# Where the stationary operands begin: 76 bytes instead of 88 or 0 into their buffers

## The chip, the cores and the metric

The kernel runs on one core of a Trainium2 chip. The metric is the time of one execution on the device in microseconds; the median of three runs is given, and beside it the profile of one execution of its own.

## The reference

One layer of a decoder trunk, x of 256 positions by 1024 features, all in float32. `proj = x @ w_in` is ten matrices of 1024 x 1024 side by side: `a_x, a_gate, s_u, s_v, q, k, v, g_a, g_s, g_m`.

- Branch A: a causal convolution of width 4 over a_x, then two gates r and i from eight 128 x 128 blocks each, `sigmoid(x @ w_r + b_r)` and the same with w_i, a linear recurrence over the positions, and a product with `gelu(a_gate)`.
- Branch B: `gelu(s_u)` times a causal 128 x 128 mixing over positions of the layer-normed `gelu(s_v)`.
- Branch C: with 256 positions and blocks of 256 this is plain causal attention with 8 heads of 128.

`merged = sigmoid(g_a) y_a + sigmoid(g_s) y_s + sigmoid(g_m) y_m`, then `x = LN(alpha x + merged @ w_out)`, then `x = LN(alpha x + ffn(x))`, where ffn has an up projection to 2 x 3072 features (gate and up), a convolution of width 3 on the gate half, gelu, product, and a down projection.

## The kernel before, in words

All large products are made in three passes of a faster float format: each operand is split into a high part `hi` (a cast on ScalarE, L70) and a low part `lo` (the difference, on VectorE, L71), and TensorE adds `hi*hi + hi*lo + lo*hi` (`passes`, L125). Weights come in chunks of 1 MB (128 partitions by 2048 numbers). A chunk is loaded into two `raw` buffers by `load` (L86, DMA queue of SyncE) and split by `prep` (L101) into one `hi` and one `lo` buffer; there are four of each, and chunks are loaded and split up to three chunks ahead of the step that uses them (`LOOK`).

TensorE's work is a list of steps in an order written out by hand (L917 on), and TensorE runs them in that order; ScalarE, VectorE and GpSimd have a planner's order, except around the first layer norm and at the end. A step is the matmuls (`pe`) and what follows them on other engines (`post`). There are these kinds:

- Feature-major steps (`fm_pe`, L219): a_x, s_u, a_gate, g_m, q, k, g_a, g_s, and the up projections of the feed-forward part. A chunk of weights is the stationary operand, 128 columns at a time, and the activations are the moving operand, 256 columns. One step is 48 matmuls at L229 (two output halves, three passes, eight blocks of k). There are 32 of them in the input projection, with x's parts `xh, xl` moving, and 22 in the feed-forward part with `x1Th, x1Tl` moving.
- Wide steps (s_v, v, w_out, down): the weights are moving, 512 columns, and the activations stationary.
- The r/i steps (`ri_step`, L410): six matmuls each, eight steps in four pairs, between the four g_m steps. Stationary are the blocks of `rg_hi, rg_lo`, moving the convolved a_x.
- Attention: scores, transposes, and `pv_step` (L562), where the halves of V, `avh, avl`, are stationary for six of ten matmuls.
- The first two gate chunks (`first_gates`, L774), where the shifted chunks are moving; constant `TM`.

Where a chunk's weights begin in its buffer is set per chunk: `shifted(i, by)` (L236) notes a number of bytes and `prep` cuts the 2048 numbers out of a buffer that is `PAD` numbers longer. Input's feature-major chunks have `FM_IN`, 88 bytes, the feed-forward's `FM_UP`, 76 bytes, all others 0. Larger activations, rg and V stand in ten slots of 8192 bytes per partition with the tag U, made by the helper `U` (L66); they begin at byte 0 of their slot. All buffers begin at multiples of 128 bytes or, for the smallest, of 32.

Of the kernel before, what the change touches and what calls it, by code (L numbers as in the profile page):

```python
# [1 line left out]

# [5 lines left out]
F32 = mybir.dt.float32  # L8
F32R = mybir.dt.float32r
# [7 lines left out]
P = 128  # L17
D = 1024
S = 256
KT = D // P  # L20
# [23 lines left out]

FM_IN, FM_UP, TM = 88, 76, 76
PAD = 256


@with_exitstack
def trunk_kernel(ctx: ExitStack, tc, xT, x, w_in, wrg, wsT, w_out, w_up, w_down, rows, packed, out):
# [7 lines left out]
    up = ctx.enter_context(tc.tile_pool(name="up", bufs=10))  # L60
# [2 lines left out]
    psa = ctx.enter_context(tc.tile_pool(name="psa", bufs=4, space=bass.MemoryType.PSUM))  # L63
    psb = ctx.enter_context(tc.tile_pool(name="psb", bufs=4, space=bass.MemoryType.PSUM))

    def U(name, shape=(P, KT, S), dt=F32):  # L66
        return up.tile(list(shape), dt, name=name, tag="U")

    def split(src, hi, lo, sub=nc.vector):
        nc.scalar.copy(hi, src)  # L70
        sub.tensor_sub(lo, src, hi.bitcast(F32))  # L71
# [14 lines left out]
    def load(i):  # L86

        parts = loaded[i] = []
        if i == 0:
            loaded["x"] = U("xraw")  # L90
        raw = [raws.tile([P, 1024], F32, name=f"raw{i}{h}", tag="raw") for h in range(2)]
        w = 512 if i < 4 else 1024
        for at in range(0, 2048, w):
            k = 2 * i + at // 1024 if i < 4 and at % 1024 == 0 else None
            if k is not None:
                nc.sync.dma_start(loaded["x"][:, k, :], xT[:, k, :])
            r = raw[at // 1024][:, at % 1024 : at % 1024 + w]
            nc.sync.dma_start(r, chunks[i][:, at : at + w])
            parts.append((r, slice(at, at + w), k))

    def prep(i):  # L101
        at = shift_of.get(i, 0) // 4
        hi = his.tile([P, 2048 + PAD], F32R, name=f"hi{i}", tag="hi")[:, at : at + 2048]
        lo = los.tile([P, 2048 + PAD], F32R, name=f"lo{i}", tag="lo")[:, at : at + 2048]
        ready[i] = (hi, lo)
# [172 lines left out]


    va = U("va", (P, 2, D))  # L280
    vst = small.tile([P, 2, 2, 6], F32, name="vst", tag="vst", bufs=1)
    psv = {}

    def sv_post():
        gb = U("gb", (P, 2, D))
        load_row(gb[:, 0, :], 0)
        load_row(gb[:, 1, :], 1)
        for tok in range(2):
            for h in range(2):
                nc.scalar.activation(va[:, tok, HALVES[h]], psv[tok, h], AF.Gelu_apprx_tanh)  # L290
                nc.vector.bn_stats(vst[:, tok, h, :], va[:, tok, HALVES[h]])
        for tok in range(2):
            mv, rs = aggregate(vst[:, tok], f"sv{tok}")
            normalise(va[:, tok, :], va[:, tok, :], mv, rs, gb[:, 0, :], gb[:, 1, :])
# [18 lines left out]
    rg = {}  # L313

    def load_rg():
        hi = U("rg_hi", (P, 2, KT, P), F32R)
        lo = U("rg_lo", (P, 2, KT, P), F32R)
        for m in range(2):
            raw = raws.tile([P, KT, P], F32, name=f"rg_raw{m}", tag="raw")
            nc.sync.dma_start(raw.rearrange("p g j -> p (g j)"), wrg[:, m * D : (m + 1) * D])  # L320
            split(raw, hi[:, m], lo[:, m])
        rg["h"], rg["l"] = hi, lo
# [142 lines left out]
    av = {}  # L465
# [1 line left out]
    pv = {}  # L467

    def v_post():
        av["h"] = U("avh", (P, 2, D), F32R)  # L470
        av["l"] = U("avl", (P, 2, D), F32R)
        av["r"] = U("avr", (P, D))
        for tok in range(2):
            for h, s in enumerate(HALVES):
                split(pv[tok, h], av["h"][:, tok, s], av["l"][:, tok, s])
                if tok == 1:
                    nc.scalar.copy(av["r"][:, s], pv[tok, h])

    def v_step(c):
        wide_step(V_, c, "p_v", pv, v_post)  # L480
# [439 lines left out]
    ax_step(0)  # L920
    ax_step(1)
    post_only(load_rg)
    ax_step(2)
    ax_step(3)
# [168 lines left out]
```

## Time and profile before

| | us |
|---|---|
| median of 3 runs | 480.73 |
| lowest, highest | 479.95, 480.8 |
| profiled execution | 479.52 |
| its span, first to last instruction | 477.6 |

The granted clock is 0.995 of the full one over the span. By the page, TensorE is busy for 98% of the span, VectorE for 70%, ScalarE for 57%. The feature-major line L229 and the row line L635 hold most of TensorE's time. In the timeline of an engine, a row is a run of equal instructions that follow one another: its start, the time from the first's start to the last's end, and how many. The rows of two runs overlap, since matmuls are pipelined; so the distance between two starts is the measure of how fast TensorE gets on, not the busy time.

### The profile page before, as it was taken

How to read it: one execution, taken by the hardware profiler on the slowest of the kernel's cores; microseconds unless marked ns; L12 is line 12 of the kernel's file. 1: busy time of each engine (PE TensorE's matmuls, PEld its weight loads, DVE VectorE, ACT ScalarE, POOL GpSimd, SP SyncE). 2: the span in 40 equal slices, each digit the busy share in tenths (PEclk: the TensorE clock that was granted, in tenths of full speed). 3: DMA queues.
4: the chain of work that ended last, by engine and by line, in shares of the span. 5: the costliest groups of instructions: out<-in, count | busy, mean ns of one | idle time of the engine just before them, and what ended most of it. 6: DMA issues, size and time to landing. Idle time of an engine off the chain costs nothing.

```text
span 477.6 us, 8706 instructions
## 1 busy us (share of the span) xinstructions
PE 467.3 (98%) x3536; PEld 443.6 (93%) x3536; DVE 336.3 (70%) x519; ACT 271.5 (57%) x400; POOL 21.8 (5%) x24
## 2 busy tenths in 40 slices
PE   8999999999999999999999999999999999999993
PEld 6899999999889999999998899999999999999983
DVE  4799989464389868676685988765666556666635
ACT  5665775576795577577451478545544454444431
POOL 1002000000000000000000800000000000000003
PEclk9999999999999999999999999999999999999998
DMA  7996868574522875765452449766556566555002
GB/s 243 355 349 247 276 209 271 182 242 150 175 82 102 251 267 184 241 245 168 141 178 90 152 139 324 276 216 202 189 178 204 196 181 212 182 185 185 26 0 88
DMA packets 27959, 92.91 MB, mean 195 GB/s; under 512 B 3216, under 2 KB 4624, under 8 KB 27920
## 3 DMA queue, kind: packets, MB, share of 16 engines
q1 hardware_dynamic: 27920, 92.37, 58.3%
q8 instruction: 27, 0.44, 0.4%
q14 instruction: 12, 0.10, 0.1%
HBM read 91.31 MB, written 1.05 MB: 193 GB/s over the span
## 4 chain that ended last, share of the span: by engine, by line
issue 46%; PE 46%; DVE 3%; ACT 1%; DMA 1%; POOL 1%; SPq 0%; ACTq 0%; DVEq 0%; POOLq 0%
PE p_u L229 14%; PE p_d L635 13%; PE p_g L229 11%; PE p_sv L265 4%; PE p_tg L247 2%; PE p_ax L229 1%; DMA raw<-in_w_in 1%; PE p_dq L635 1%; ACT hi L70 1%; DVE lo L71 0%; DVE va L206 0%; DVE st_m L193 0%; POOL rs_sv L201 0%; DVE x1Tl L71 0%; POOL rs_m L201 0%
## 5 line engine op out<-in xcount | busy, mean ns | idle before, releaser
L71 DVE TENSOR_TENSOR lo<-raw,hi 128x1024 fp32r<-128x1024 f32 (+1 forms) x165 | 191.3, 1183 | 71.4 <-ACT hi L70 70.7
L70 ACT CAST hi<-raw 128x1024 fp32r<-128x1024 f32 (+1 forms) x167 | 162.9, 1008 | 100.9 <-PE p_g L229 26.3
L635 PE MATMUL p_d<-hi,act 128*128 128x512 f32 x180 | 55.6, 390 | 0.0
L635 PEld LDWEIGHTS p_d<-hi,act 128*128 128x128 f32 x180 | 33.0, 188 | 6.3
L635 PE MATMUL p_d<-lo,act 128*128 128x512 f32 x90 | 35.0, 389 | 0.0
L329 DVE SCALAR_TENSOR_TENSOR cv<-p_g,par,cv 128x255 f32<-128x255 f32 (+1 forms) x48 | 23.1, 480 | 7.1 <-ACT cv L327 6.3
L229 PE MATMUL p_u<-x1Th,hi 128*128 128x256 f32 x192 | 26.0, 278 | 0.0
L229 PE MATMUL p_u<-x1Th,lo 128*128 128x256 f32 x192 | 25.7, 276 | 0.0
L229 PE MATMUL p_u<-x1Tl,hi 128*128 128x256 f32 x192 | 25.7, 276 | 0.0
L229 PEld LDWEIGHTS p_u<-x1Th,hi 128*128 128x128 f32 x192 | 24.5, 188 | 0.8
L327 ACT ACTIVATE cv<-p_g,par 128x256 f32<-128x256 f32 x24 | 13.5, 562 | 19.9 <-DVE cv L329 19.8
L229 PEld LDWEIGHTS p_u<-x1Th,lo 128*128 128x128 f32 x192 | 23.6, 188 | 0.0
L229 PEld LDWEIGHTS p_u<-x1Tl,hi 128*128 128x128 f32 x192 | 23.5, 188 | 0.0
L767 DVE TENSOR_TENSOR cv<-cv,p_u 128x512 f32<-128x512 f32 x12 | 8.2, 687 | 19.2 <-PE p_u L229 19.2
L229 PE MATMUL p_g<-x1Th,lo 128*128 128x256 f32 x160 | 21.4, 276 | 0.0
L229 PE MATMUL p_g<-x1Th,hi 128*128 128x256 f32 x160 | 21.4, 276 | 0.0
L229 PE MATMUL p_g<-x1Tl,hi 128*128 128x256 f32 x160 | 21.4, 276 | 0.0
L635 PEld LDWEIGHTS p_d<-lo,act 128*128 128x128 f32 x90 | 16.9, 188 | 3.6
L229 PEld LDWEIGHTS p_g<-x1Th,lo 128*128 128x128 f32 x160 | 19.6, 188 | 0.0
L229 PEld LDWEIGHTS p_g<-x1Th,hi 128*128 128x128 f32 x160 | 19.6, 188 | 0.0
L229 PEld LDWEIGHTS p_g<-x1Tl,hi 128*128 128x128 f32 x160 | 19.6, 188 | 0.0
L751 ACT ACTIVATE cv<-cv 128x512 f32<-128x512 f32 x12 | 7.6, 632 | 11.3 <-DVE cv L329 11.3
(242 smaller groups left out, 934.8 us busy)
## 6 DMA issues: line engine op xcount, KB each, us to landing
raw<-in_w_in SPq DMA_DIRECT2D x72, 512.0 KB, 5.3
raw<-in_w_up SPq DMA_DIRECT2D x48, 512.0 KB, 4.6
raw<-in_w_down SPq DMA_DIRECT2D x24, 512.0 KB, 4.9
raw<-in_w_in SPq DMA_DIRECT2D x16, 256.0 KB, 5.2
raw<-in_w_out SPq DMA_DIRECT2D x8, 512.0 KB, 3.9
xraw<-in_xT SPq DMA_DIRECT2D x8, 128.0 KB, 4.7
gb<-in_rows SPq DMA_DIRECT2D x2, 512.0 KB, 6.6
rg_raw<-in_wrg SPq DMA_DIRECT2D x2, 512.0 KB, 6.9
```

The costliest lines, as they stand in the source:

```text
L70: nc.scalar.copy(hi, src)
L71: sub.tensor_sub(lo, src, hi.bitcast(F32))
L229: nc.tensor.matmul(dst[:, j, :], w[:, k, j * P : (j + 1) * P], a[:, k, :], start=(n == 0), stop=(n == 3 * KT - 1))
L247: nc.tensor.matmul(dst, a[:, k, tok * P : (tok + 1) * P], w[:, k, :], start=(m == 0 and k == 0), stop=(m == 2 and k == KT - 1))
L265: nc.tensor.matmul(tiles[tok, h], a[:, 2 * c + k, tok * P : (tok + 1) * P], w[:, k, HALVES[h]], start=(c == 0 and k == 0 and m == 0), stop ...
L327: nc.scalar.activation(dst, src, AF.Identity, bias=pcol(bname, f), scale=w(taps - 1))
L329: nc.vector.scalar_tensor_tensor(dst[:, d:], src[:, : S - d], w(taps - 1 - d), dst[:, d:], op0=ALU.mult, op1=ALU.add)
L635: nc.tensor.matmul(dst, a[:, k0 + k, tok * P : (tok + 1) * P], w[:, k, s], start=(start and n == 0), stop=(stop and n == 6 * len(parts) - 1))
L751: nc.scalar.activation(t, t, AF.Gelu_apprx_tanh)
L767: nc.vector.tensor_mul(t, t, pf["u", c])
```

## The change

`FM_IN` becomes 76. A new constant `STAT`, 76, is the byte at which rg's and V's high and low parts begin in their slots; for that `U` takes a number of bytes, makes each slot 2048 + 32 numbers long, cuts the wanted numbers out and gives them their shape. `PAD` goes from 256 to 128 numbers. All buffers behind the first pair of weight buffers come to stand elsewhere, the slots of U 8320 bytes apart in place of 8192.

```diff
-FM_IN, FM_UP, TM = 88, 76, 76
-PAD = 256
+FM_IN, FM_UP, TM = 76, 76, 76
+
+STAT = 76
+PAD = 128
...
-    def U(name, shape=(P, KT, S), dt=F32):
-        return up.tile(list(shape), dt, name=name, tag="U")
+    def U(name, shape=(P, KT, S), dt=F32, by=0):
+
+        t = up.tile([P, 2048 + 32], dt, name=name, tag="U")[:, by // 4 : by // 4 + math.prod(shape[1:])]
+        axes = "abcd"[: len(shape) - 1]
+        return t.rearrange(f"p ({' '.join(axes)}) -> p {' '.join(axes)}", **dict(zip(axes, shape[1:])))
...
-        hi = U("rg_hi", (P, 2, KT, P), F32R)
-        lo = U("rg_lo", (P, 2, KT, P), F32R)
+        hi = U("rg_hi", (P, 2, KT, P), F32R, STAT)
+        lo = U("rg_lo", (P, 2, KT, P), F32R, STAT)
...
-        av["h"] = U("avh", (P, 2, D), F32R)
-        av["l"] = U("avl", (P, 2, D), F32R)
+        av["h"] = U("avh", (P, 2, D), F32R, STAT)
+        av["l"] = U("avl", (P, 2, D), F32R, STAT)
```

## Rows read from the trace of the kernel before

**Rows 1.** The page, parts 1 and 2: busy time of engines, granted clock by slice.
```profile
PE 467.3 (98%) x3536; PEld 443.6 (93%) x3536; DVE 336.3 (70%) x519; ACT 271.5 (57%) x400; POOL 21.8 (5%) x24
...
PEclk9999999999999999999999999999999999999998
```

**Rows 2.** TensorE's waits: for whom, us in total, times, longest.
```profile
PE p_x1t L675 <- DVE x L725: 0.7, 1, 0.7
PE p_su L229 <- DVE xc L329: 0.3, 1, 0.3
```

**Rows 3.** TensorE's timeline (start, us, line, matmuls), fast steps: second a_x, first g_m.
```profile
33.41 1.07 PE L229 MATMUL p_ax<-xh,hi 128*128 128x256 f32 x8
...
38.85 1.07 PE L229 MATMUL p_ax<-xh,hi 128*128 128x256 f32 x8
...
97.83 1.07 PE L229 MATMUL p_gm<-xh,hi 128*128 128x256 f32 x8
...
103.28 0.28 PE L416 MATMUL p_ri<-xch,rg_hi 128*128 128x256 f32 x1
```

**Rows 4.** The same timeline, second u step and its successor.
```profile
55.65 1.20 PE L229 MATMUL p_su<-xh,hi 128*128 128x256 f32 x8 [0.32 <-DVE xc L329]
...
61.48 1.06 PE L377 MATMUL p_mix<-ws_raw,va 128*128 128x128 f32 x8
```

**Rows 5.** The same timeline: second g_m step, from behind one r/i pair to the next.
```profile
104.71 1.10 PE L229 MATMUL p_gm<-xh,hi 128*128 128x256 f32 x8
...
110.31 0.28 PE L416 MATMUL p_ri<-xch,rg_hi 128*128 128x256 f32 x1
```

**Rows 6.** The same timeline: first a_gate step, first g_s step, each with its successor.
```profile
75.02 1.19 PE L229 MATMUL p_ag<-xh,hi 128*128 128x256 f32 x8
...
80.58 1.05 PE L377 MATMUL p_mix<-ws_raw,va 128*128 128x128 f32 x8
...
224.12 1.18 PE L229 MATMUL p_gs<-xh,hi 128*128 128x256 f32 x8
...
229.80 0.40 PE L569 MATMUL p_o<-pT,avh 128*128 128x256 f32 x2
```

**Rows 7.** Stretches: us, TensorE busy (matmuls), granted clock, DMA share, GB/s.
```profile
33.41:38.84 5.43, 5.43 (x50) 1.00 1.02 404
104.71:110.30 5.59, 5.59 (x50) 1.00 0.67 215
```

**Rows 8.** TensorE's timeline, feed-forward: u steps behind transposes and behind a down step.
```profile
283.64 1.19 PE L229 MATMUL p_u<-x1Th,hi 128*128 128x256 f32 x8
...
289.21 0.60 PE L809 MATMUL p_g<-ident,tg 128*128 128x128 f32 x4
...
306.03 1.08 PE L229 MATMUL p_u<-x1Th,hi 128*128 128x256 f32 x8
...
311.48 1.07 PE L229 MATMUL p_g<-x1Th,hi 128*128 128x256 f32 x8
```

**Rows 9.** Timelines of ScalarE, then TensorE, around the start of V's projection.
```profile
123.66 2.00 ACT L70 CAST hi<-raw 128x1024 fp32r<-128x1024 f32 x2 [3.09 <-PE p_gm L229]
...
127.12 0.49 ACT L424 ACTIVATE i<-p_ri,par 128x256 f32<-128x256 f32 x1
...
126.76 0.62 PE L265 MATMUL p_v<-lo,xh 128*128 128x512 f32 x2
127.22 0.94 PE L265 MATMUL p_v<-hi,xh 128*128 128x512 f32 x2
```

**Rows 10.** TensorE's timeline, one step of probabilities times V and its successor.
```profile
194.56 0.40 PE L569 MATMUL p_o<-pT,avh 128*128 128x256 f32 x2
...
195.73 0.39 PE L512 MATMUL p_s<-kf,qf 128*128 128x128 f32 x2
```

**Rows 11.** VectorE's groups by line, 82 to 103 us, then 300 to 440 us.
```profile
L71 DVE TENSOR_TENSOR lo<-raw,hi 128x1024 fp32r<-128x1024 f32 x8 | 9.5, 1221 | 2.7 <-ACT hi L70 2.7
...
L71 DVE TENSOR_TENSOR lo<-raw,hi 128x1024 fp32r<-128x1024 f32 x53 | 63.2, 1221 | 30.7 <-ACT hi L70 30.6
```

More of the change, by code (lines that the diff above doesn't have):

```diff
@@ L1 @@
+import math
 from contextlib import ExitStack
```

## The prediction

> **What bounds the kernel now.** I read part 1 and part 2 of the page first: TensorE is busy for 98% of the span and its clock is at the upper level (2.4 GHz) in every slice but the last [rows 1]. The waits of TensorE came next: the longest inside the input projection is 0.3 us, for the convolution on VectorE in front of the second u step, and the one for the second layer norm's rows in front of the transposes 0.7 us [rows 2]. So nearly all the time is the spacing of matmuls, and the question is whether that spacing is the same wherever the same instruction runs. For this I took TensorE's timeline and divided the distance between the starts of two steps by the matmuls between them. One feature-major step is 48 matmuls of 256 columns, with the weights stationary and the activations moving.
>
> The second a_x step takes 38.85 - 33.41 = 5.44 us, the first g_m step 103.28 - 97.83 = 5.45 us: 113.3 ns a matmul [rows 3]. The second u step, with the same 48 instructions and the same 88 bytes, takes 61.48 - 55.65 = 5.83 us, 121.5 ns a matmul with a long first distance of some 0.2 us in it and 120 ns without [rows 4]. The three later g_m steps take 110.31 - 104.71 = 5.60 us (the first of three equal ones), 116.7 ns a matmul, and the r/i steps around them, whose weights begin at byte 0 of their slots, take (104.71 - 103.28) / 12 = 119 ns [rows 5]. The first g_s step takes 229.80 - 224.12 = 5.68 us where the first a_gate step, which also follows 128-column matmuls, takes 80.58 - 75.02 = 5.56 us [rows 6]. So there are three spacings, 113, 117 and 120 ns, and once a step has a slow one it keeps it. It isn't the clock, which is granted in full in both, nor the DMA: the fast step ran beside 404 GB/s, a slow one beside 215 GB/s [rows 7].
>
> The feed-forward steps have their weights 76 bytes in. The first u step there, entered after transposes as the first g_s step is, begins with a block that is 0.12 us longer and then settles: 289.21 - 283.64 = 5.57 us; after a down step it is 311.48 - 306.03 = 5.45 us [rows 8]. I found no step with 76 bytes stationary that stays slow, among 22 of them; with 88 bytes five of 32 do (the second u, three g_m, one g_s), and with 0 bytes every r/i step.
>
> **The change part by part.** It adds no instruction and no transfer. It moves three things: the start of 32 weight chunks from byte 88 to 76, the start of the r/i weights and of V's two halves from byte 0 to 76, and, through the smaller pad and the larger slots, the base of all buffers behind the first pair. The bases stay multiples of 128 bytes.
>
> *The second u step.* Its entry is dear anyway (the wait, then a long first distance), so I don't take 5.44 but the 5.56 us of the first a_gate step: 5.83 - 5.56 = 0.27 us. Ends: 0 if it stays at 120 ns, 0.39 at the full 5.44.
>
> *The g_m steps.* Three times 5.60 - 5.44 = 0.48 us. They follow the r/i steps and seem to inherit their slowness. Ends: 0 and 0.48; I take 0.48, since both the matmuls before them and they themselves move to the offset of [rows 8].
>
> *The r/i steps.* 48 matmuls from about 119.7 to 113.3 ns: 0.30 us. Ends: 0 and 0.30. Of this the last pair is not kept. After it the V projection waits for a PSUM bank that ScalarE frees: two casts from 123.66 on (released by TensorE's last reading of the weights two thirds through the last g_m step), then a sigmoid and four more at 0.36 us. TensorE's first block after that is 0.94 us in place of 0.62 [rows 9]. ScalarE's chain doesn't shorten, so TensorE only comes some 0.1 us earlier to the same wait: minus 0.10.
>
> *The first g_s step.* 5.68 - 5.56 = 0.12 us. Ends 0 and 0.12.
>
> *Probabilities times V.* A step is ten matmuls in 195.73 - 194.56 = 1.17 us [rows 10]; six have V's halves stationary, of which two or three come before the 128-column pair that breaks the rhythm. Four steps with two matmuls at 6.7 ns less give 0.05 us. Ends: 0 and 24 x 6.7 ns = 0.16 us.
>
> *Writing at another offset.* VectorE's subtraction into a weight buffer takes 1221 ns at 88 bytes and 1221 ns in the feed-forward part, where 76 and 0 bytes alternate [rows 11]; I cost the writes at nothing, and what hides them anyway is that TensorE never waits for a weight buffer there. If VectorE were late, the second u step's wait of 0.3 us would grow first.
>
> Two statements of the Trainium skill speak against this. "TensorE: Matmul & The Clock Gate", section "Step-by-step: what each phase is for", says that TensorE reads moving and stationary operands through two independent ports, so that loading the next weights takes nothing from the running matmul; by that the bytes could not matter and the sum would be 0. The trace disagrees so far as the same instruction has three spacings, 113, 117 and 120 ns [rows 3 to 6]. "SBUF — State Buffer", section "Specifications (TRN2)", says that memory is read in lines of 16 bytes and that every crossing costs; 76 isn't a multiple of 16, so that by it the r/i weights and V would read one line more and lose, and the sum would be at most 0.87 us without these two. Here too the trace disagrees: the weights at byte 0 have the longest spacing, 119 ns [rows 5].
>
> **Sum:** 0.27 + 0.48 + 0.30 - 0.10 + 0.12 + 0.05 = 1.12 us. TensorE is what ends last before and after, so the saving reaches the end of the span, and the layer norms, which hang on TensorE's last matmul before them, move along. The profiled execution has a span of 477.6 and took 479.52 us, 1.2 us under the median of 480.73; the saving is taken off the median: 479.6 us.
>
> **The rivals.** *Entry decides, not the bytes.* With 88 bytes eight steps entered after 128-column matmuls settle, the first a_gate step [rows 6] being one of them, so the slow ones may be accidents of the phase at which TensorE starts, and 76 bytes have been seen after only two kinds of entry. Then the r/i steps at 113 ns still hand the g_m steps a fast start, but the second u and the first g_s step stay: 0.48 + 0.30 - 0.10 + 0.05 = 0.73, 480.0 us. Against it: all 22 steps at 76 bytes settle. *Nothing moves:* the spacing hangs on something else, say on the order of banks, and the r/i steps stay at 119 ns: 480.7 us; the steps with 76 bytes are then fast for another reason than their bytes, and for that speaks only that most steps with 88 are fast too. By the first statement of the Trainium skill above it would be this case. *Slower:* slots of 8320 bytes in place of 8192 move the activations of the feed-forward part by multiples of 128 bytes against the weights, which no row of the trace has tried. If conflicts repeat at 256 or 512 bytes rather than at 128 or less, the 22 up steps lose their 113 ns. At 116.7 ns each costs 0.16 us: 22 x 0.16 = 3.5 us against 1.12, 483.1 us; from the eighth step on (7 x 0.16 = 1.12) the kernel is slower. For it: these steps hold 120 us. Against it: in the address plan of the kernel before, x in the input part and the activations in the feed-forward part stand 256 bytes apart, counted modulo 512, and both reach 113.3 ns [rows 3, 8]. *More:* the entries after 128-column matmuls, nine of them at about 0.12 us, settle sooner: up to 0.5 us more, 479.1 us.
>
> **How the numbers follow.** Forecast 0.50, entry 0.20, nothing 0.13, slower 0.10, more 0.07. A difference under 0.2%, 0.96 us, can hardly be told from none here, and my 1.12 us is just above it: I count 0.40 of the forecast's 0.50 as faster, all of the last case and 0.03 of the second. That gives faster 0.50, same 0.40, slower 0.10. The range runs from 478.8 (all upper ends, 0.39 + 0.48 + 0.30 + 0.12 + 0.16 = 1.45, and half a microsecond of drift between medians, since the three runs spread by 0.85) to 481.0 (nothing moves, with drift); it leaves out the slower case.
>
> **What would show it.** Right: the second u step at 5.56 us, all four g_m steps at 5.44, r/i steps at 1.36 us for twelve matmuls, the first g_s step at 5.56, and the wait in front of V about 0.1 us longer. Wrong: any of these at its old length, or a feed-forward up step over 5.46 us.

## The result and the profile after

The changed kernel takes 484.8 us (median of 4, 484.67 to 486.23) against 480.74 (median of 4): a ratio of 1.009, with an interval of 1.0069 to 1.011. It is slower by 4.1 us; 479.6 was forecast. The time is that of the rival called *Slower* (483.1 us, chance 0.10), and 1.7 us more.

The page looks as before: TensorE is busy for 98% of a longer span, and its granted clock is at the upper level (2.4 GHz) in every slice but the last.

```profile
PE 474.0 (98%) x3536; PEld 449.6 (93%) x3536; DVE 336.8 (70%) x519; ACT 271.7 (56%) x400; POOL 21.7 (4%) x24
...
PEclk9999999999999999999999999999999999999998
```

First the input projection, TensorE's timeline of the changed kernel (start, us, line, matmuls): the second u step, the second g_m step from behind its r/i pair, the first g_s step, each with the row behind it, which answer to [rows 4 to 6].

```profile
57.29 1.15 PE L235 MATMUL p_su<-xh,hi 128*128 128x256 f32 x8 [0.33 <-DVE xc L335]
62.81 0.61 PE L383 MATMUL p_mix<-ws_raw,va 128*128 128x128 f32 x4
...
104.49 0.28 PE L422 MATMUL p_ri<-xch,rg_hi 128*128 128x256 f32 x1
...
105.91 1.10 PE L235 MATMUL p_gm<-xh,hi 128*128 128x256 f32 x8
111.38 0.28 PE L422 MATMUL p_ri<-xch,rg_hi 128*128 128x256 f32 x1
...
224.82 1.20 PE L235 MATMUL p_gs<-xh,hi 128*128 128x256 f32 x8
230.39 0.40 PE L575 MATMUL p_o<-pT,avh 128*128 128x256 f32 x2
```

62.81 - 57.29 = 5.52 us where it was 5.83; 111.38 - 105.91 = 5.47 where it was 5.60; 230.39 - 224.82 = 5.57 where it was 5.68. The r/i pair, 105.91 - 104.49 = 1.42 us, is almost as slow as before.

Then the feed-forward part, the timeline of one gate step in blocks of eight matmuls, with the down step behind it; it answers to the second half of [rows 8].

```profile
346.99 1.12 PE L235 MATMUL p_g<-x1Th,hi 128*128 128x256 f32 x8
347.95 1.10 PE L235 MATMUL p_g<-x1Tl,hi 128*128 128x256 f32 x8
348.88 1.11 PE L235 MATMUL p_g<-x1Th,lo 128*128 128x256 f32 x8
349.83 1.12 PE L235 MATMUL p_g<-x1Th,hi 128*128 128x256 f32 x8
350.79 1.10 PE L235 MATMUL p_g<-x1Tl,hi 128*128 128x256 f32 x8
351.73 1.11 PE L235 MATMUL p_g<-x1Th,lo 128*128 128x256 f32 x8
352.68 0.62 PE L641 MATMUL p_d<-hi,act 128*128 128x512 f32 x2
```

The step takes 352.68 - 346.99 = 5.69 us, 0.24 more than before, with the same 76 bytes and not one instruction changed. What changed is where the activations lie: in the address plan (the places at which the build puts the buffers) x1Th has come to byte 0 modulo 256 and x1Tl to byte 128; before, both lay at 128, as x does in the input part. The weights' buffers begin at 128 modulo 256 in both kernels, so the weights at 128 + 76 = 204. And the blocks show it: where x1Tl is moving, eight matmuls take 348.88 - 347.95 = 0.93 us, and the last three of them are back at 113 to 114 ns; where x1Th is moving, eight take 0.95 to 0.96 us and stay at about 119 to 120 ns on average.

All of it by stages, each from the starts of its steps in the timelines of the two profiled executions (us, after minus before):

| stage | difference | forecast |
|---|---|---|
| second u step | -0.31 | -0.27 |
| four steps entered after 128-column matmuls (u, a_gate) | -0.12 | - |
| r/i steps, eight | -0.08 | -0.30 |
| wait in front of V | +0.06 | +0.10 |
| later g_m steps, three | -0.41 | -0.48 |
| probabilities times V, four | -0.11 | -0.05 |
| first g_s step | -0.11 | -0.12 |
| output projection, up to its last quarters | +0.35 | 0 |
| feed-forward steps of 48 matmuls, 22 | +5.27 | 0 |
| down steps | +0.71 | 0 |
| all other steps from the first a_x on | -0.18 | 0 |

From the first matmul of the first a_x step to the start of the last matmul it is 446.86 us against 441.79, 5.07 us more. The medians lie only 4.1 us apart. The start of the first a_x step differs between executions by more than that 1 us: 27.45 to 29.59 us in the profiles of this study, and 29.42 against 27.45 in e2 and e10a below, whose kernels are equal up to there. That this explains the whole of the 1 us isn't shown. So the stretch from there on is given below beside the medians.

### The profile page after: what moved, and what is told of

It is laid out like the page before. It is cut to its first block, busy times and chain, and to the rows that moved or that the text cites. A ratio compares the mean times of both kernels' runs of the same rounds, so it can differ in the third digit from the quotient of the medians.

```text
span 484.3 us, 8706 instructions
## 1 busy us (share of the span) xinstructions
PE 474.0 (98%) x3536; PEld 449.6 (93%) x3536; DVE 336.8 (70%) x519; ACT 271.7 (56%) x400; POOL 21.7 (4%) x24
## 4 chain that ended last, share of the span: by engine, by line
PE 48%; issue 46%; DVE 3%; ACT 1%; DMA 1%; POOL 1%; ACTq 0%; SPq 0%; DVEq 0%; POOLq 0%
PE p_u L235 14%; PE p_d L641 13%; PE p_g L235 12%; PE p_sv L271 5%; PE p_tg L253 2%; PE p_ax L235 1%; PE p_dq L641 1%; DMA raw<-in_w_in 1%; ACT hi L76 1%; DVE lo L77 0%; DVE va L212 0%; DVE st_m L199 0%; POOL rs_sv L207 0%; DVE x1Tl L77 0%; POOL rs_m L207 0%
## 5 line engine op out<-in xcount | busy, mean ns | idle before, releaser
L235 PE MATMUL p_u<-x1Th,hi 128*128 128x256 f32 x192 | 27.0, 282 | 0.0
L235 PE MATMUL p_u<-x1Th,lo 128*128 128x256 f32 x192 | 26.7, 281 | 0.0
L235 PE MATMUL p_g<-x1Th,hi 128*128 128x256 f32 x160 | 22.4, 282 | 0.0
```

What stands on the lines that cost most here:

```text
L235: nc.tensor.matmul(dst[:, j, :], w[:, k, j * P : (j + 1) * P], a[:, k, :], start=(n == 0), stop=(n == 3 * KT - 1))
```

## The experiments

The theory after the result, called A in the expectations: what counts is how many bytes the stationary weights stand beyond the moving activations, modulo 256. At 76 matmuls of 256 columns settle at 113.3 ns. The slots of 8320 bytes, 128 more than a multiple of 256, put every second activation at another distance. Rivals: the 76 bytes themselves, the smaller pad, or the slots' length as such. One more rival stands untested: that not the distance counts but each operand's own place modulo 256. Every step that kept 113.3 ns at a distance of 76 had its weights at 204 and its activations at 128; no run moved both operands of such a whole step by the same number of bytes. What follows is told in distances, as the expectations are, and bears either reading.

| kernel | median, us | before beside it | first a_x to last matmul |
|---|---|---|---|
| before | | | 441.79 |
| changed | 484.8 | 480.74 | 446.86 |
| e1: slots of 8320 alone | 486.41 | 480.48 | 448.08 |
| e2: changed, slots of 8448 | 479.52 | 480.48 | 440.73 |
| e3: before, feed-forward weights at 204 | 491.31 | 480.48 | 451.93 |
| e4: changed, x1Th moved by 128 | 479.45 | 480.48 | 442.04 |
| e6: before, Input at 76 | 479.68 | 480.43 | 441.65 |
| e8: slots of 8448, r/i and V at 76 | 480.44 | 480.43 | 441.73 |
| e3b: before, feed-forward weights at 332 | 479.4, one run | 480.43 | 441.53 |
| e3c: before, feed-forward weights at 140 | 487.01, one run | 480.43 | 449.33 |
| e10a: e2, first gate chunks at 180 | 479.74 | 480.61 | 440.77 |
| e10b: e10a, act and mg at 76 | 480.66 | 480.61 | 442.49 |

The second u step's wait for VectorE was longer in the profiled executions of e4, e6 and e2 (the step ahead of it 6.57, 6.72 and 6.11 us against 5.92), which is 0.65, 0.80 and 0.19 us of their last column.

**e1, the slots alone.**

```diff
-FM_IN, FM_UP, TM = 76, 76, 76
+FM_IN, FM_UP, TM = 88, 76, 76
-STAT = 76
+STAT = 0
```

> Changed kernel with the offsets of before (88 bytes for Input's weights, 0 for r/i weights and V): only the slots of 8320 bytes and the smaller pad are left. Theory A (stationary weights and moving activations must stand the same number of bytes apart modulo 256; slots 128 bytes apart modulo 256 break this in the feed-forward part): the 20 later feed-forward steps of 48 matmuls stay at 5.69 us, every second down step at 5.57, and none of Input's gains: 1.3 us over the changed kernel, about 486 us. Theory B (the 76 bytes do it): feed-forward steps back at 5.44 to 5.46, 480.7 us.

486.41 us, ratio 1.0117 (1.0097 to 1.0137). The groups by line of e1 (count, busy us, mean ns of one):

```profile
L235 PE MATMUL p_g<-x1Th,hi 128*128 128x256 f32 x160 | 22.4, 282 | 0.0
L235 PE MATMUL p_g<-x1Tl,hi 128*128 128x256 f32 x160 | 22.0, 280 | 0.0
```

The ten later gate steps take 56.92 us together, as in the changed kernel, against 54.40 before, and the down steps and the output projection lose the same 0.71 and 0.35 us. So without any of the change's 76-byte edits the whole loss is there. The expectation that all of Input's gains would be gone was wrong: the three later g_m steps ran at 5.45 us and the first g_s step at 5.56 with their weights at 88, and the four steps of probabilities times V won the same 0.11 us with V's halves at 0. The a_gate steps three and four and the first g_m step, which had run at 5.44, took 5.60. 88 bytes give either spacing.

**e2, slots of 8448.**

```diff
-        t = up.tile([P, 2048 + 32], dt, name=name, tag="U")[:, by // 4 : by // 4 + math.prod(shape[1:])]
+        t = up.tile([P, 2048 + 64], dt, name=name, tag="U")[:, by // 4 : by // 4 + math.prod(shape[1:])]
```

> Changed kernel with slots of 8448 bytes in place of 8320, so that all slots begin at the same byte modulo 256; everything else as changed. Theory A: feed-forward steps back to 5.44 to 5.46, all down steps at 5.47, w_out back, r/i pairs at 1.36 to 1.38 us for twelve matmuls, Input's gains kept: 479.4 to 479.8 us, faster than before by 0.9 to 1.3. Theory B (only the first place, at multiples of 512, is good, or the smaller pad did it): still over 484 us.

479.52 us, ratio 0.9977 (0.9965 to 0.999): faster than before by about 1 us, and A's time. The pad is still the smaller one, so it isn't the cause. The groups by line of e2 (count, busy us, mean ns of one): at 256 columns a mean of 276 ns goes with the spacing of 113 ns, 280 and more with a slower one.

```profile
L641 PE MATMUL p_d<-hi,act 128*128 128x512 f32 x180 | 55.6, 390 | 0.0
L235 PE MATMUL p_g<-x1Th,hi 128*128 128x256 f32 x160 | 21.4, 276 | 0.0
L641 PE MATMUL p_wo<-hi,mgh 128*128 128x512 f32 x28 | 10.9, 389 | 0.0
L422 PE MATMUL p_ri<-xch,rg_hi 128*128 128x256 f32 x16 | 4.4, 276 | 0.0
```

The same view of the changed kernel:

```profile
L641 PE MATMUL p_d<-hi,act 128*128 128x512 f32 x180 | 56.1, 393 | 0.0
L235 PE MATMUL p_g<-x1Th,hi 128*128 128x256 f32 x160 | 22.4, 282 | 0.0
L641 PE MATMUL p_wo<-hi,mgh 128*128 128x512 f32 x28 | 11.1, 396 | 0.0
L422 PE MATMUL p_ri<-xcl,rg_hi 128*128 128x256 f32 x16 | 4.5, 282 | 0.0
```

In e2 a pair of r/i steps takes 1.36 us for twelve matmuls, the forecast length; in the changed kernel (1.42 us) the slots put xch, xcl and the r/i weights at distances of 204 and 76 in turn.

**e3, e3b, e3c: only the feed-forward weights moved, in the kernel before.**

```diff
-FM_IN, FM_UP, TM = 88, 76, 76
+FM_IN, FM_UP, TM = 88, 204, 76
```

(332 and 140 in the other two.)

> Kernel before with one number changed: the feed-forward weights begin 204 bytes into their buffers in place of 76, that is 128 further; slots, pad and all else as before. Theory A: the x1Th and x1Tl blocks both get the slow spacing of the changed kernel's x1Th blocks, 118 to 120 ns a matmul, 5.68 to 5.76 us a step, 22 steps by 0.24 to 0.32: 486 to 488 us. Theory B (slots or pad as such): 480.7.

> Kernel before with the feed-forward weights 332 bytes in, 76 + 256. Theory A (only the distance modulo 256 counts): every feed-forward step as before, 5.44 to 5.46 us, 480.5 us. Theory B (the distance counts modulo 512 or more, or as a length): steps of 5.6 to 5.9 us, 484 us and more.

> Kernel before with the feed-forward weights 140 bytes in, 76 + 64. If the distance counts modulo 64, the steps stay at 5.44 to 5.46 us and the time at 480.5; if modulo 128 or 256, they needn't: 5.6 to 5.9 us a step, 484 to 491 us. Theory A (256) leaves it open how bad 140 is, and expects it to differ from 76.

Mean ns of one in the groups by line, first of e3, then e3b, then e3c:

```profile
L229 PE MATMUL p_g<-x1Th,hi 128*128 128x256 f32 x160 | 23.0, 286 | 0.0
L229 PE MATMUL p_g<-x1Tl,hi 128*128 128x256 f32 x160 | 23.0, 286 | 0.0
```

```profile
L229 PE MATMUL p_g<-x1Th,hi 128*128 128x256 f32 x160 | 21.4, 276 | 0.0
L229 PE MATMUL p_g<-x1Tl,hi 128*128 128x256 f32 x160 | 21.4, 276 | 0.0
```

```profile
L229 PE MATMUL p_g<-x1Tl,hi 128*128 128x256 f32 x160 | 22.4, 282 | 0.0
L229 PE MATMUL p_g<-x1Th,hi 128*128 128x256 f32 x160 | 22.4, 282 | 0.0
```

At 204 bytes the time is 491.31 us, ratio 1.0225 (1.0203 to 1.0247); at 332 it is that of before; at 140, 487.01. So 256 bytes more change nothing, 128 and 64 more do: of the lengths tried the distance counts modulo 256. I had the size at 204 wrong, 486 to 488: a gate step takes 59.20 / 10 = 5.92 us, 123.3 ns a matmul, a fourth spacing that I hadn't seen. Here both activations stand at the bad distance, in the changed kernel only x1Th; that the x1Tl blocks are what holds the changed kernel at 5.69 us is likely, but not shown. Of the 7.5 us that e3c has more in the last column, 0.8 lie in its input part, though nothing is changed there: its a_gate steps three and four and its first g_m step took 5.60 us, as in e1, in place of 5.44.

**e4, one activation.**

```diff
-res["hl"] = [U(f"x1T{x}", dt=F32R) for x in "hl"]
+res["hl"] = [U(f"x1T{x}", dt=F32R, by=128 * (x == "h")) for x in "hl"]
```

> Changed kernel with one activation moved: x1Th begins 128 bytes into its slot, so that it stands as x1Tl does modulo 256; slots of 8320 bytes stay. Theory A: the 22 feed-forward steps fall back to 5.44 to 5.56 us, 5.2 us less, while every second down step and w_out stay slow: 479.4 to 480 us. Theory B (slots of 8320 bytes are bad as such, or the pad): 484.8 us, no change.

479.45 us, ratio 0.9986 (0.9972 to 1.0001). The groups of e4 show the gate steps at the fast spacing, the output projection still slow:

```profile
L235 PE MATMUL p_g<-x1Th,lo 128*128 128x256 f32 x160 | 21.4, 276 | 0.0
L641 PE MATMUL p_wo<-hi,mgh 128*128 128x512 f32 x28 | 11.1, 396 | 0.0
```

Every second down step stays at 5.56 us. So 128 bytes on one buffer give back 5.3 us, with slots of 8320 and the small pad in place, and slots and pad as such are ruled out as the cause in these steps.

**e6, Input at 76 alone.**

```diff
-FM_IN, FM_UP, TM = 88, 76, 76
+FM_IN, FM_UP, TM = 76, 76, 76
```

> Kernel before with one number changed: Input's feature-major weights 76 in place of 88 bytes in; r/i weights and V at 0, slots of 8192 bytes. Theory A (76 bytes settle from any entry, 88 only from some): the second u step 5.52 to 5.54 us, the first g_s step 5.57, and the three g_m steps behind the slow r/i pairs 5.44 to 5.48, though the r/i pairs stay at 1.44; 0.9 us in all: 479.6 us. Theory B (the g_m steps inherit the r/i steps' slowness whatever their own bytes): the g_m steps stay at 5.60, 0.4 us in all: 480.1.

479.68 us, ratio 0.998 (0.9966 to 0.9995). The timeline of e6, the start and the end of the second g_m step:

```profile
105.40 1.08 PE L229 MATMUL p_gm<-xh,hi 128*128 128x256 f32 x8
...
110.85 0.28 PE L416 MATMUL p_ri<-xch,rg_hi 128*128 128x256 f32 x1
```

The second u step takes 5.54 us, the first g_s step 5.53, the three g_m steps 5.45 each, though the r/i pairs in front of them stay at 1.44. So 76 bytes settle from a slow entry too; theory B falls. In the six profiled kernels that have Input at 76 no feature-major step of the input projection stays slow.

**e8, r/i and V at 76, Input left at 88.** e2 with one number changed:

```diff
-FM_IN, FM_UP, TM = 76, 76, 76
+FM_IN, FM_UP, TM = 88, 76, 76
```

> Slots of 8448 bytes, r/i weights and V at 76 bytes, Input's weights left at 88. Theory A: r/i pairs at 1.36 us and with them the three g_m steps at 5.44, since they are entered at the fast spacing; second u step stays at 5.83 and the first g_s step is free to fall either way (5.56 or 5.68): 0.8 us in all, 479.7 us. Theory B (88 bytes are slow by themselves behind r/i steps): g_m steps stay at 5.60, 480.1.

480.44 us, ratio 1.0007 (0.9994 to 1.002): no change, where 479.7 was expected. The first half of A holds, r/i pairs at 1.36 us and the g_m steps at 5.44. But the first two g_a steps, which had run at 5.56 and 5.44 in the kernel before, have fallen into the 120 ns spacing. The timeline of e8, blocks of eight 0.96 us apart through both steps:

```profile
201.11 1.12 PE L235 MATMUL p_ga<-xh,hi 128*128 128x256 f32 x8
202.07 1.12 PE L235 MATMUL p_ga<-xl,hi 128*128 128x256 f32 x8
203.03 1.12 PE L235 MATMUL p_ga<-xh,lo 128*128 128x256 f32 x8
203.99 1.12 PE L235 MATMUL p_ga<-xh,hi 128*128 128x256 f32 x8
```

They take 5.84 and 5.76 us, and with the first g_s step at 5.84 they eat up 0.76 of the 0.80 us won. Together with e1 this shows that at 88 bytes both spacings hold themselves. That the way in which TensorE enters a run of steps decides is the reading nearest to it, but no run isolates an entry. It isn't the kernel alone: e3, e3b and e3c have the input part of the kernel before unchanged, and the second u step took 5.83, 5.55 and 5.68 us there. So a part of what the changed kernel seems to win in that step can come without any change.

**e10a and e10b, further on the same road from e2.**

```diff
-FM_IN, FM_UP, TM = 76, 76, 76
+FM_IN, FM_UP, TM = 76, 76, 180
```

and in e10b also (the new lines alone)

```diff
+            act = U(f"act{c}", (P, 2, 2, S), F32R, STAT)
+                mg["h"] = U("mgh", dt=F32R, by=STAT)
+                mg["l"] = U("mgl", dt=F32R, by=STAT)
```

> Slots of 8448 bytes with 76 for Input, r/i and V, and the first gate chunks, which are the moving operand there, 180 bytes in (256 - 76) in place of 76, so that the stationary activations stand 76 bytes beyond them modulo 256. If only the distance stationary minus moving counts: the 96 gate matmuls go from 118 to 113.3 ns where nothing breaks in, some 0.3 us less, about 479.2 us. If moving operands must begin at byte 0, or the sign doesn't matter: no change from the slots of 8448 alone, 479.5.

> As e10a, and the activations that are stationary in the down and output projections (act, mgh, mgl) 76 bytes in as well. The last 36 matmuls of 256 columns and the 24 of the output projection's last quarters go from 120 to 113.3 ns: 0.4 us less, about 478.8 us. The 270 matmuls of 512 columns at 226.7 ns shouldn't move if their weights' load hides behind them at any distance; if 76 bytes disturb them as 128 did, every down step costs 0.1 us more and the gain is lost.

e10a: 479.74 us, ratio 0.9973 (0.996 to 0.9985), no different from e2. The 96 gate matmuls with their weights moving took 12.63 us against 12.48. One of their groups, in e10a and then in e2:

```profile
L253 PE MATMUL p_tg<-hi,x1Tl 128*128 128x256 f32 x32 | 6.0, 284 | 0.0
```

```profile
L253 PE MATMUL p_tg<-hi,x1Tl 128*128 128x256 f32 x32 | 5.9, 279 | 0.0
```

The distance is now 76 and they aren't faster, so the distance stationary minus moving is not the whole rule: here the moving operand begins at 52 modulo 256 and the stationary at 128, where the fast steps have 128 and 204. At neither of the two places tried for these moving weights, 204 and 52, did the matmuls settle at 113 ns. e10b: 480.66 us, ratio 1.0005 (0.9991 to 1.0019). Its groups show both ends:

```profile
L641 PE MATMUL p_d<-hi,act 128*128 128x512 f32 x180 | 56.5, 395 | 0.0
L641 PE MATMUL p_dq<-hi,act 128*128 128x256 f32 x24 | 4.2, 277 | 0.0
```

The last matmuls of 256 columns fall from 283 to 277 ns and win 0.35 us with the output projection's, as expected; those of 512 columns rise from 390 to 395 and lose 1.45 us in the down steps and 0.52 in the output projection. At 512 columns, distances of 0 and 256 are the good ones and 76 and 128 aren't.

By the stretch from the first a_x step on, e2 is the shortest (440.73 us), with e10a beside it; by their medians e2, e4, e6 and e10a can't be told apart.

## Why the prediction was wrong

*Where the time is* was right: TensorE's spacing, on three levels, and e3 has a fourth at 123.3 ns.

*Input's gains* were right in sum, -1.08 us measured over the rows of the table down to the first g_s step against -1.12 forecast with its minus for V, but that the two are so near is in part luck. The r/i steps gave 0.08 in place of 0.30, because the new slots put their operands at different distances; e2, where all stand at 76, gives the 1.36 us a pair. Four entries after 128-column matmuls made up 0.12, which stood among the rivals as *More*, and probabilities times V gave 0.11 in place of 0.05, which can't be put down to V's 76 bytes, since e1 has it with V at 0. That the g_m steps inherit the slowness fits e8, but e1 has them at 5.45 us at 88 bytes behind r/i pairs of 1.42; at 76 it isn't needed (e6). The r/i weights at byte 0 were also not the slowest, as the prediction says in one place: the second u step at 88 bytes has the same 120 ns.

*The step that failed* is the cost of moving all other buffers. The prediction wrote "The bases stay multiples of 128 bytes" and let that stand for no cost; the runs show that 128 bytes cost and 256 don't (e3, e3b), and that the longer slots alone bring the whole loss (e1). Its own sign of being wrong, a feed-forward up step over 5.46 us, came with 5.68 to 5.78. The rival *Slower* named exactly this mechanism and place, and got 0.10. What was set against it, that x in the input part and the feed-forward activations lie 256 bytes apart modulo 512 and both run at 113.3 ns, was true, but it tests 256 and says nothing on 128, the distance that the change brought in. No row tested 128, so the bound should have been weighed as open, and with 120 us of such steps behind it the chance was far too small. Its price was too small as well: 0.16 us a step was taken from the 117 ns level, 0.24 came; and it left out the wide steps, 0.71 us in the down steps and 0.35 in the output projection, whose stationary activations moved too.

*The Trainium skill's two statements* were rightly not followed, and on the first the runs go further. By "TensorE: Matmul & The Clock Gate", section "Step-by-step: what each phase is for", of the Trainium skill, loading the next weights takes no read bandwidth from the running matmul. The prediction drew from it that the bytes could not matter; e3, one number away from the kernel before, is 10.1 us longer from the first a_x step to the last matmul. No run shows which part of the memory or of TensorE is shared. That the two reads collide is a reading that fits, since moving either operand alone does it (e3 the weights, the longer slots x1Th), but it isn't shown.

## What to carry to other kernels

When a change moves buffers, look up each pair of operands that one instruction reads and compare their starting bytes before and after, modulo more than you believe to matter; a helper that makes every slot a little longer moves all of them. Divide the distance between the starts of steps by the matmuls in them: equal instructions at unequal spacing are a finding even if the engine is 98% busy. Look at the same step in more than one profile before you call a spacing its own: the second u step had three lengths in four executions of one unchanged input part. A bound that no row tests is open, and what it would cost grows with all the work that depends on it.

## What the hardware showed that I had not expected

- With matmuls of 256 columns in the kernel's faster float format (float32r) the spacing depends on where the two operands begin, and 256 bytes more make no difference. By the distance of the stationary operand beyond the moving one, modulo 256, with the moving one at 128: 113.3 ns at 76 in every step that has only this distance; 113, 117 or 120 at 88, not always the same in the same step; 119 to 120 at 0; 123 at 204; 119.7 at 140 (5.74 us a gate step). With the moving operand at 52 a distance of 76 was slow too (e10a, 121.7 ns in its last 48 gate matmuls), so the distance alone isn't the rule.
- A spacing holds itself: in e8 two whole steps at 88 bytes ran at 120 ns, 96 matmuls, until another kind of instruction broke in.
- At 512 columns the spacing is 227 ns at distances of 0 and 256, and 232 to 233 at 128 and 76 (the changed kernel's down steps, 5.48 against 5.58 us; e10b, 5.59).
